# Attention by one query block of a pair of heads, with float32 value products and shortened low-part products

## Chip, cores and metric

The kernel runs on one core of a Trainium2 chip. The metric is the device time of one execution in microseconds. Five engines work side by side, each through its own queue in order: PE (matrix products; PEld is its loading of the stationary operand), DVE (elementwise and scans, also out of PSUM), ACT (activations and copies), POOL (elementwise on SBUF) and SP (here it only issues DMAs).

## What is computed

One layer of a hybrid encoder on 2048 tokens of width 1024, in float32: a norm, one input projection whose columns feed an attention group and a recurrent group, an output projection, a gated FFN with a convolution. 16 learned tokens are put before the sequence (T = 2064). The change touches the attention, for 8 heads of 64:

```python
z = einsum("bhqd,bhkd->bhqk", qb, kb) * scale
mask = s_pos < t_pos
log_keep = where(mask, log_sigmoid(-z), 0.0)
after = cumsum(log_keep, axis=3, reverse=True) - log_keep
w = where(mask, exp(log_sigmoid(z) + after), 0.0)
out = einsum("bhqk,bhkd->bhqd", w, vb)
```

## The kernel before, in words

The time axis is cut into a block of 16 tokens and 16 blocks of 128. Most products split a float32 operand into a high and a low part of the type fp32r and multiply the parts in single passes: `mm3` (L107) is high·high, high·low and low·high.

- **Projections.** For each pair of heads j, q and k go to DRAM as parts (`qd`, `kd`: the first index is high or low), v as float32 (`vd`).
- **Load of a head** (`load_head`, L115). Rows 0 to 63 of `K2` hold the high part of k, rows 64 to 127 the low part. A weight w is the difference of two neighbouring running products of keep probabilities, so the kernel multiplies the running products by differences of neighbouring v rows and adds one row of v at the end (L594). `dv` holds these differences, split by POOL into a high and a low half (L136, L137).
- **Query-key products** (`products_of`, L555). A unit is a pair of query blocks of one head. `q2` holds q twice, in both halves of the rows, so one product over 128 rows multiplies a part of q with high and low k together: L569 for the high part of q, L570 for the low part. A chunk is at most 512 keys. ACT turns it into keep probabilities (L571); DVE forms their running product backwards over one or two chunks (L578 with the mask, L580 without).
- **Value products** (`outputs_of`, `flush`, L600 to L642). PE transposes blocks of 128 x 128 (`transpose`, L97) into PSUM, two query blocks beside each other. For each group of up to 512 columns ACT copies the high part (L585) and DVE subtracts it to get the low part (L586). Each 128 keys need two products of up to 256 columns (L612), with high and low `dv` side by side in the 128 columns of the stationary operand. The two halves of the result are stored apart (`od`, L596) and are added later in `mix` (L526).
- **Order.** Units come in the order of L661, the products of one unit ahead of the outputs of the unit before. A scheduler orders each engine's queue when the program is built; the queues then run in that order. PSUM has three banks `m` for query-key products, one `v` for outputs, and two each of `t` and `u` for transposes.
- **After the attention** come the output projection with `mix` (L521, L767) and the FFN (L876 and the products L108 to L110 into `bk`).

Of the kernel before, what the change touches and what calls it, by code (L numbers as in the profile page):

```python
# [16 lines left out]
P = 128  # L17
META = 16
# [37 lines left out]
def hymba_block(  # L56
# [22 lines left out]
    od = {g: dram.tile([2, 4, P, META if g < 0 else 2 * P], F32, name=f"od{g + 1}") for g in range(-1, NT // 2)}  # L79
# [32 lines left out]
    heads = {}  # L112
    hb_stack = ExitStack()

    def load_head(hd, hb):  # L115
        j, hh = hd // 2, hd % 2
        rows = slice(hh * HD, hh * HD + HD)
        K2 = hb.tile([P, T], F32R, name="K2", tag="K2")
        dv = hb.tile([P, NT + 1, 2, HD], F32R, name="dv", tag="dv")
        nc.gpsimd.memset(f(dv[:, NT]), 0.0)  # L120
        cuts = [0, 4, 8, NT]
        for s0, s1 in zip(cuts, cuts[1:]):
            c0 = s0 * P + (META if s0 else 0)
            c1 = s1 * P + META
            for e in range(2):
                nc.sync.dma_start(f(K2[e * HD:(e + 1) * HD, c0:c1]), kd[j][e, rows, c0:c1])
            va = hb.tile([P, 9, HD], F32, name="va", tag="va")
            vb = hb.tile([P, 9, HD], F32, name="vb", tag="vb")
            m = s1 - s0
            for v, o in ((va, 1), (vb, 0)):  # L130
                nc.sync.dma_start(v[:, :m], vd[j][o + s0 * P:o + s1 * P, hh].rearrange("(s p) d -> p s d", p=P))
                if s1 == NT:
                    nc.sync.dma_start(v[:META, m], vd[j][o + NT * P:o + T, hh])
            parts = [(P, u, u + 4) for u in range(0, m, 4)] + ([(META, m, m + 1)] if s1 == NT else [])
            for n, u0, u1 in parts:
                nc.gpsimd.tensor_tensor(vb[:n, u0:u1], vb[:n, u0:u1], va[:n, u0:u1], op=ALU.subtract)  # L136
                split_pool(dv[:n, s0 + u0:s0 + u1, 0], dv[:n, s0 + u0:s0 + u1, 1], vb[:n, u0:u1])  # L137

        vl = hb.tile([NT + 1, HD], F32, name="vl", tag="vl")
        nc.sync.dma_start(vl[0:1], vd[j][META:META + 1, hh])  # L140
        nc.sync.dma_start(vl[1:], vd[j][META + P:1 + T:P, hh])
        vlT = hb.tile([P, NT + 1], F32, name="vlT", tag="vlT")
        nc.gpsimd.memset(vlT[HD:], 0.0)
        return j, rows, K2, dv, vlT, vl
# [24 lines left out]
    with ExitStack() as A:  # L169
# [332 lines left out]
        def before(j, i):  # L502
            if j == 2 and i == 0:
                heads[0] = load_head(0, hbE)
# [16 lines left out]
    def mix(mH, mL, src, t0, n):  # L521

        g, c0 = (-1, 0) if t0 < META else divmod(t0 - META, 2 * P)
        for a, d in enumerate((od[g][0, :, :, c0:c0 + n], od[g][1, :, :, c0:c0 + n], old[:, :, t0:t0 + n])):
            nc.sync.dma_start(src[a], d.rearrange("k p t -> p k t"))
        nc.vector.tensor_tensor(src[0], src[0], src[1], op=ALU.add)  # L526
        for ks, m in ((slice(0, 4), src[0]), (slice(4, 8), src[2])):
            nc.scalar.copy(mH[:, ks], m)
            nc.vector.tensor_tensor(mL[:, ks], m, f(mH[:, ks]), op=ALU.subtract)
# [4 lines left out]
    with ExitStack() as B:  # L534
# [10 lines left out]
        G = 2  # L545
        LOW = META + 8 * P

        def load_q(head, t0, n):
            j, rows = head[:2]
            q2 = hq.tile([P, 2, G * P], F32R, name="q2", tag="q2", bufs=4)  # L550
            for e in range(2):
                nc.sync.dma_start(f(q2[e * HD:(e + 1) * HD, :, :n]), qd[j][:, rows, t0:t0 + n].rearrange("s d t -> d s t"))
            return q2

        def products_of(head, i, q2, qc):  # L555

            K2 = head[2]
# [3 lines left out]
            kp = (wl if low else wk).tile([P, (LOW if low else T) + 112], F32, name="kp", tag="kp", bufs=4)  # L561
            if i >= 0:
                nc.gpsimd.memset(kp[:, n:n + 112], 0.0)  # L563
            sizes = chunks_of(n)
            hi = n
            for ci, sz in enumerate(sizes):
                c0 = hi - sz if ci == 0 else c0 - sz
                zt = acc_bank()
                nc.tensor.matmul(zt[:rn, :sz], lhsT=q2[:, 0, qc:qc + rn], rhs=K2[:, c0:c0 + sz], start=True, stop=False)  # L569
                nc.tensor.matmul(zt[:rn, :sz], lhsT=q2[:, 1, qc:qc + rn], rhs=K2[:, c0:c0 + sz], start=False, stop=True)  # L570
                nc.scalar.activation(kp[:rn, c0:c0 + sz], zt[:rn, :sz], AF.Sigmoid, scale=-0.125)  # L571
                if ci % 2 and c0:
                    continue
                rev = kp[:rn, c0:hi][:, ::-1]
                if hi == n:

                    m0 = 512 - P + rn - sz
                    nc.vector.tensor_tensor_scan(rev, rev, mask[:rn, m0:m0 + sz][:, ::-1], initial=1.0, op0=ALU.mult, op1=ALU.max)  # L578
                else:
                    nc.vector.tensor_tensor_scan(rev, rev, rev, initial=kp[:rn, hi:hi + 1], op0=ALU.mult, op1=ALU.bypass)  # L580
                hi = c0
            return kp

        def evac(h, l, src):
            nc.scalar.copy(h, src)  # L585
            nc.vector.tensor_tensor(l, src, f(h), op=ALU.subtract)  # L586

        def store_o(head, av, i0, t0, m):
            j, rows, vlT = head[0], head[1], head[4]
            ov = a1.tile([P, G * P], F32, name="qn", tag="qn", bufs=2)  # L590
            for c in range(0, m, P):
                e = min(c + P, m)
                b = i0 + 1 + c // P
                nc.scalar.activation(ov[:, c:e], av[:, c:e], AF.Identity, bias=vlT[:, b:b + 1])  # L594
            for a in range(2):
                nc.sync.dma_start(od[i0 // G][a, j, rows, :m], ov[a * HD:(a + 1) * HD, :m])  # L596
# [3 lines left out]
        def flush(head, av, pend, cols, pt, nj):  # L600
            dv = head[3]
            nflush[0] += 1
            if nflush[0] % 2:
                tH = a1.tile([P, 2, 256], F32R, name="qk", tag="qk", bufs=2).rearrange("p a t -> p (a t)")
            else:
                tH = wk.tile([P, 512], F32R, name="tH", tag="tH", bufs=2)
            tL = wk.tile([P, 512], F32R, name="tL", tag="tL", bufs=4)
            pp = pend[0][2]
# [7 lines left out]
        def outputs_of(head, g, kps):  # L616
            if g < 0:
                pt = tu_bank()
                transpose(pt[:META, :META], kps[0][:META, :META])
                av = pmv.tile([P, 2, 256], F32, name="v", tag="v")[:, 0]  # L620
                flush(head, av, [(0, 0, META, 0, META)], META, pt, 1)
                store_o(head, av, -1, 0, META)
                return
            i0 = g * G
            av = pmv.tile([P, 2, 256], F32, name="v", tag="v")[:, 0]
            nj = i0 + G + 1
            pend, cols = [], 0
            pt = tu_bank()
            for s in range(nj):
                first = max(0, s - 1 - i0)  # L630
                nn = (G - first) * P
                if cols + nn > 512:
                    flush(head, av, pend, cols, pt, nj)
                    pt = tu_bank()
                    pend, cols = [], 0
                for b in range(first, G):
                    c = cols + (b - first) * P
                    transpose(pt[:, c:c + P], kps[b][:, s * P:(s + 1) * P])
                pend.append((s, first * P, P, cols, nn))
                cols += nn  # L640
            flush(head, av, pend, cols, pt, nj)
            store_o(head, av, i0, META + i0 * P, G * P)  # L642

        def make_products(head, g):
            if g < 0:
                return [products_of(head, -1, load_q(head, 0, META), 0)]
            q2 = load_q(head, META + g * G * P, G * P)
            return [products_of(head, g * G + b, q2, b * P) for b in range(G)]
# [3 lines left out]


        def finish_head(head):

            vlT, vl = head[4:]
            pt = tu_bank()
            transpose(pt[:HD, :NT + 1], vl)
            nc.vector.tensor_copy(vlT[:HD], pt[:HD, :NT + 1])
# [354 lines left out]
```

## Time and profile before

| what | value |
|---|---|
| runs of the kernel before | 2718.18, 2722.47, 2722.88 us (median 2722.47) |
| profiled execution: its own time / its span | 2722.01 us / 2720.3 us |
| busy over the span: PE, PEld, DVE, ACT, POOL | 94%, 84%, 66%, 46%, 44% |
| mean granted clock of TensorE | 0.981 of 2.4 GHz |
| first to last scan of the attention (L578, L580) | starts from 583.3 to 1110.3 us |
| last value product (L612) starts | 1126.1 us |

The page's line of 40 slices shows which engine is full in which stage: PE in the projections and in the FFN, DVE with a 9 in every slice from the ninth to the sixteenth, which is the attention. A matmul's shown duration reaches from its start to its modelled end, and the next one starts before that; the distance between two starts is what one costs in a row.

### The profile page before, as it was taken

The page shows a single profiled execution, that of the slowest core. Times are in us where ns is not written, and L with a number is a line of the kernel's source. Part 1 is how long each engine was busy: PE and PEld are TensorE (multiplying, and loading weights), DVE is VectorE, ACT ScalarE, POOL GpSimd, SP SyncE. Part 2 cuts the span into 40 slices and gives each one's busy share as a digit, 9 for nine tenths or more (in the row PEclk, how much of TensorE's full clock was granted, in tenths as well). Part 3 has the DMA queues.
Part 4 walks back from the last instruction along what each step waited for, and adds up shares of the span by engine and source line. Part 5 has one row for each costly group of instructions (what it writes and reads, how often), then busy time and mean ns, then how long its engine had stood idle before and what let it go on. Part 6 is the DMA issues. An engine that isn't in the chain of part 4 may idle for free. (4 is left out here: it accounts for less than half of the span.)

```text
span 2720.3 us, 40399 instructions
## 1 busy us (share of the span) xinstructions
PE 2563.3 (94%) x15012; PEld 2293.5 (84%) x15012; DVE 1802.9 (66%) x2080; ACT 1241.5 (46%) x2331; POOL 1185.4 (44%) x1152
## 2 busy tenths in 40 slices
PE   7998889988888888999899999999999999999999
PEld 6998889977777778788799999988788888887887
DVE  5678853259999999655677667553745666665443
ACT  4355532246666666432355454432434545453221
POOL 4455564434522321000265555534456665653443
PEclk9999989999999999999899999999999999999999
DMA  5311143243333321577322222244653222225463
GB/s 157 111 33 33 45 113 98 76 113 96 102 81 85 83 78 50 138 222 223 108 86 71 91 74 78 86 159 146 208 169 109 79 84 79 85 79 172 141 211 109
DMA packets 316860, 296.41 MB, mean 109 GB/s; under 512 B 62182, under 2 KB 269270, under 8 KB 316662
## 3 DMA queue, kind: packets, MB, share of 16 engines
q1 hardware_dynamic: 316662, 293.82, 35.5%
q8 instruction: 118, 1.93, 0.3%
q14 instruction: 80, 0.66, 0.1%
HBM read 211.68 MB, written 82.07 MB: 108 GB/s over the span
## 5 line engine op out<-in xcount | busy, mean ns | idle before, releaser
L876 PE MATMUL bk<-mb,wt 128*128 128x258 f32 (+2 forms) x5544 | 878.8, 321 | 11.5 <-ACT u L906 2.3
L876 PEld LDWEIGHTS bk<-mb,wt 128*128 128x128 f32 x5544 | 794.9, 190 | 95.4 <-DVE c L910 3.2
L705 POOL TENSOR_TENSOR wt<-wst,wt 128x512 fp32r<-128x512 f32 (+1 forms) x264 | 485.5, 1845 | 488.8 <-ACT wt L704 263.6
L705 DVE TENSOR_TENSOR wt<-t,wt 128x512 fp32r<-128x512 f32 x88 | 173.4, 1973 | 213.0 <-ACT wt L704 213.0
L108 PE MATMUL bk<-wt 128*128 128x512 f32 x704 | 276.4, 394 | 8.0 <-ACT wt L704 8.0
L109 PE MATMUL bk<-wt 128*128 128x512 f32 x704 | 276.6, 393 | 0.0
L110 PE MATMUL bk<-wt 128*128 128x512 f32 x704 | 271.9, 391 | 4.2 <-DVE wt L705 4.2
L704 ACT CAST wt<-wst 128x512 fp32r<-128x512 f32 (+1 forms) x264 | 200.1, 762 | 121.3 <-PE bk L876 111.8
L705 POOL TENSOR_TENSOR wt<-ss,wt 128x512 fp32r<-128x512 f32 x132 | 197.0, 1495 | 121.7 <-ACT wt L704 120.4
L580 DVE TENSOR_TENSOR_SCAN kp<-kp 128x456 f32<-128x456 f32 (+6 forms) x144 | 238.2, 1655 | 0.9
L612 PE MATMUL v<-tL,dv 128*128 128x256 f32 (+1 forms) x648 | 178.7, 300 | 43.5 <-DVE tL L586 42.4
L938 DVE SCALAR_TENSOR_TENSOR t<-c,fw,t 128x1024 f32<-128x1024 f32 x88 | 135.1, 1535 | 116.0 <-ACT t L937 116.0
L571 ACT ACTIVATE kp<-m 128x388 f32<-128x388 f32 (+13 forms) x360 | 169.0, 508 | 70.7 <-PE m L570 39.7
L704 ACT CAST wt<-t 128x512 fp32r<-128x512 f32 x88 | 54.6, 621 | 281.2 <-PE bk L110 231.4
L612 PEld LDWEIGHTS v<-tL,dv 128*128 128x128 f32 x648 | 125.6, 194 | 59.1 <-DVE tL L586 57.4
L108 PEld LDWEIGHTS bk<-wt 128*128 128x128 f32 x704 | 133.9, 190 | 37.0 <-ACT wt L704 9.0
L110 PEld LDWEIGHTS bk<-wt 128*128 128x128 f32 x704 | 132.8, 189 | 33.0 <-DVE wt L705 5.5
L109 PEld LDWEIGHTS bk<-wt 128*128 128x128 f32 x704 | 133.9, 190 | 27.9
L940 DVE SCALAR_TENSOR_TENSOR c<-c,fw,t 128x1024 f32<-128x1024 f32 x88 | 154.0, 1750 | 3.0
L563 POOL MEMSET kp<- 128x112 f32 x128 | 23.7, 190 | 285.0 <-PE t L97 130.9
L569 PE MATMUL m<-K,q 128*128 128x452 f32 (+12 forms) x360 | 143.2, 399 | 2.5 <-ACT kp L571 2.2
L578 DVE TENSOR_TENSOR_SCAN kp<-kp,mask 128x388 f32<-128x388 f32 (+15 forms) x136 | 130.3, 968 | 0.1
(300 smaller groups left out, 5508.1 us busy)
## 6 DMA issues: line engine op xcount, KB each, us to landing
wst<-in_w_ffn_in_dram SPq DMA_DIRECT2D x88, 512.0 KB, 4.1
wst<-in_w_ffn_out_dram SPq DMA_DIRECT2D x88, 512.0 KB, 5.4
pd<-c SPq DMA_DIRECT2D x44, 512.0 KB, 3.3
t<-pd SPq DMA_DIRECT2D x88, 256.0 KB, 3.5
q<-qd SPq DMA_DIRECT2D x128, 128.0 KB, 2.8
wst<-in_w_in_dram SPq DMA_DIRECT2D x48, 192.0 KB, 2.8
xt<-in_x_dram SPq DMA_DIRECT2D x16, 512.0 KB
od<-qn SPq DMA_DIRECT2D x128, 64.0 KB, 2.1
```

What stands on the lines that cost most here:

```text
L108: nc.tensor.matmul(ps, lhsT=sH, rhs=mH, start=first, stop=False)
L109: nc.tensor.matmul(ps, lhsT=sH, rhs=mL, start=False, stop=False)
L110: nc.tensor.matmul(ps, lhsT=sL, rhs=mH, start=False, stop=last)
L569: nc.tensor.matmul(zt[:rn, :sz], lhsT=q2[:, 0, qc:qc + rn], rhs=K2[:, c0:c0 + sz], start=True, stop=False)
L571: nc.scalar.activation(kp[:rn, c0:c0 + sz], zt[:rn, :sz], AF.Sigmoid, scale=-0.125)
L580: nc.vector.tensor_tensor_scan(rev, rev, rev, initial=kp[:rn, hi:hi + 1], op0=ALU.mult, op1=ALU.bypass)
L612: nc.tensor.matmul(av[:, q0:q0 + nn], lhsT=dv[:pp, s].rearrange("p a d -> p (a d)"), rhs=tt[:pp, c:c + nn], start=(s == 0 and half == 0), ...
L704: nc.scalar.copy(h, src)
L705: low.tensor_tensor(l, src, f(h), op=ALU.subtract)
L876: nc.tensor.matmul(ps_, lhsT=s, rhs=m, start=first and k == 0 and n_ == 0, stop=k == 3 and n_ == 2, skip_group_check=True)
L938: nc.vector.scalar_tensor_tensor(t, c_[:, HALO - 1:HALO - 1 + PHW], pf[:, 1:2], t, op0=ALU.mult, op1=ALU.add)
L940: nc.vector.scalar_tensor_tensor(c_[:, uv], c_[:, uv], pf[:, 0:1], t, op0=ALU.mult, op1=ALU.add)
```

## The change

It has five parts.

1. A unit is one query block of a pair of heads. `load_pair` makes two tiles `K2[e]`, one per head: for head 0 the high part of k lies in rows 0 to 63, for head 1 in rows 64 to 127, the low part in the other half.
2. The high part of q still meets both parts of k over 128 rows. The low part of q meets the high part of k alone, over 64 rows: rows 0 to 63 for head 0, rows 64 to 127 for head 1 (L572). The product of the two low parts is left out.
3. The transposed products are copied as float32, by ACT or, for the second head of each fifth group, by DVE. There is no low part, and the subtract L586 is gone.
4. `dv` stays float32 and is not split. A value product has a stationary operand of 64 columns and 128 moving columns, both float32: head 0 writes partitions 0 to 63 of the bank, head 1 partitions 64 to 127 (L611).
5. The output is whole, so it is stored once per unit, and `mix` loads one table less and adds nothing.

```diff
+        K2 = [hb.tile([P, T], F32R, name=f"K2{e}", tag=f"K2{e}") for e in range(2)]
+        dv = hb.tile([P, NT + 1, 2, HD], F32, name="dv", tag="dv")
...
             for e in range(2):
-                nc.sync.dma_start(f(K2[e * HD:(e + 1) * HD, c0:c1]), kd[j][e, rows, c0:c1])
...
+                for a in range(2):
+                    nc.sync.dma_start(f(K2[e][a * HD:(a + 1) * HD, c0:c1]), kd[j][a ^ e, e * HD:(e + 1) * HD, c0:c1])
...
-                split_pool(dv[:n, s0 + u0:s0 + u1, 0], dv[:n, s0 + u0:s0 + u1, 1], vb[:n, u0:u1])
...
+                nc.gpsimd.tensor_tensor(dv[:, u:u + 4], dv[:, u:u + 4], va, op=ALU.subtract)
...
-                zt = acc_bank()
-                nc.tensor.matmul(zt[:rn, :sz], lhsT=q2[:, 0, qc:qc + rn], rhs=K2[:, c0:c0 + sz], start=True, stop=False)
-                nc.tensor.matmul(zt[:rn, :sz], lhsT=q2[:, 1, qc:qc + rn], rhs=K2[:, c0:c0 + sz], start=False, stop=True)
-                nc.scalar.activation(kp[:rn, c0:c0 + sz], zt[:rn, :sz], AF.Sigmoid, scale=-0.125)
...
+                zt = [acc_bank()[:rn, :sz] for e in range(2)]
+                for e in range(2):
+                    nc.tensor.matmul(zt[e], lhsT=q2[e][:, 0], rhs=K2[e][:, cs], start=True, stop=False)
+
+                for e in range(2):
+                    r = slice(e * HD, (e + 1) * HD)
+                    nc.tensor.matmul(zt[e], lhsT=q2[e][r, 1], rhs=K2[e][r, cs], start=False, stop=True)
+                for e in range(2):
+                    nc.scalar.activation(kps[e][:rn, cs], zt[e], AF.Sigmoid, scale=-0.125)
...
-            evac(tH[:pp, :cols], tL[:pp, :cols], pt[:pp, :cols])
-            for s, q0, pp, c, nn in pend:
-                for half, tt in enumerate((tH, tL)):
                     nc.tensor.matmul(
-                        av[:, q0:q0 + nn], lhsT=dv[:pp, s].rearrange("p a d -> p (a d)"), rhs=tt[:pp, c:c + nn],
-                        start=(s == 0 and half == 0), stop=(s == nj - 1 and half == 1))
...
+                if e and nflush[0] % 5 == 1:
+                    nc.vector.tensor_copy(tT[:pp, :cols], pts[e][:pp, :cols])
+                else:
+                    nc.scalar.copy(tT[:pp, :cols], pts[e][:pp, :cols])
+                ts.append(tT)
+            for s, nn in pend:
+                c = s % 4 * P
+                for e in range(2):
+                    nc.tensor.matmul(
+                        av[e * HD:(e + 1) * HD], lhsT=dv[:pp, s, e], rhs=ts[e][:pp, c:c + nn],
+                        start=s == 0, stop=s == nj - 1)
...
+        order = (7, 15, -1, 0, 14, 1, 13, 2, 12, 3, 11, 4, 10, 5, 9, 6, 8)
```

The scheduler builds new queues from this, and the two changes of PE's queue and the one of DVE's that matter look as follows. A row has the line, the operation, output<-inputs, and for a product stationary columns x moving columns; `v` is the output bank, `m` a bank of query-key products, `t` and `u` banks of transposes, `tH`, `tL`, `tT` and `qk` the tables copied from them.

PE in the middle of the attention before, around the last value products of a unit:

```order
L612 MATMUL v_7984<-tL_7991,dv_7557 128x256
L612 MATMUL v_7984<-qk_8000,dv_7557 128x128
L612 MATMUL v_7984<-tL_8001,dv_7557 128x128
L569 MATMUL m_8377<-K2_7556,q2_8355 128x392
L570 MATMUL m_8377<-K2_7556,q2_8355 128x392
L97 MATMUL u_8122<-ident_85,kp_8014 128x128
L97 MATMUL u_8122<-ident_85,kp_8035 128x128
```

PE in the middle of the attention of the change, value products of two groups (`tT_7678` is head 0's table, `tT_7680` and `qk_7658` are head 1's):

```order
L611 MATMUL v_7601<-qk_7658,dv_6351 64x128
L611 MATMUL v_7601<-tT_7678,dv_6351 64x128
L97 MATMUL u_7691<-ident_93,kp_7553 128x128
L611 MATMUL v_7601<-tT_7680,dv_6351 64x128
L611 MATMUL v_7601<-tT_7678,dv_6351 64x128
```

A high and a low table stood in turn, each with 128 stationary columns; now the tables of the two heads stand in turn, each with 64.

PE a little further on in the change, query-key products (`K20` is head 0's, `K21` head 1's):

```order
L572 MATMUL m_8005<-K20_6349,q2_7995 128x452
L572 MATMUL m_8006<-K21_6350,q2_7998 128x452
L611 MATMUL v_7601<-qk_7694,dv_6351 64x128
L97 MATMUL t_7822<-ident_93,kp_7779 128x128 x3
L611 MATMUL v_7601<-qk_7696,dv_6351 64x128
L97 MATMUL u_7757<-ident_93,kp_7743 128x128 x2
L97 MATMUL t_7822<-ident_93,kp_7779 128x128
L97 MATMUL u_7823<-ident_93,kp_7781 128x128 x4
L568 MATMUL m_8015<-K20_6349,q2_7995 128x452
L572 MATMUL m_8015<-K20_6349,q2_7995 128x452
L568 MATMUL m_8016<-K21_6350,q2_7998 128x452
L572 MATMUL m_8016<-K21_6350,q2_7998 128x452
```

The low-part products (L572) of the two heads stand behind one another in the first two rows and apart in the last four. Over the whole queue they stand behind one another for 56 of the 180 pairs of chunks.

DVE in the middle of the attention before (the scans L578 and L580, in the change L582 and L585, are the rows with SCALAR_TENSOR_TENSOR on `kp`):

```order
L586 TENSOR_TENSOR tL_6246<-t_6240,tH_6245 128x512
L586 TENSOR_TENSOR tL_6259<-u_6253,qk_6258 128x512
L580 SCALAR_TENSOR_TENSOR kp_6542<-kp_6542 128x392
L586 TENSOR_TENSOR tL_6272<-t_6266,tH_6271 128x512
L586 TENSOR_TENSOR tL_6285<-u_6279,qk_6284 128x512
L578 SCALAR_TENSOR_TENSOR kp_6610<-kp_6610,mask_5831 128x388
L586 TENSOR_TENSOR tL_6298<-t_6292,tH_6297 128x512
L580 SCALAR_TENSOR_TENSOR kp_6610<-kp_6610 128x780
```

DVE in the attention of the change:

```order
L585 SCALAR_TENSOR_TENSOR kp_6988<-kp_6988 128x950
L604 COPY qk_6955<-t_6944 128x512
L585 SCALAR_TENSOR_TENSOR kp_6990<-kp_6990 128x950
L582 SCALAR_TENSOR_TENSOR kp_7096<-kp_7096,mask_5836 128x392
L582 SCALAR_TENSOR_TENSOR kp_7098<-kp_7098,mask_5836 128x392
L585 SCALAR_TENSOR_TENSOR kp_7096<-kp_7096 128x392
L585 SCALAR_TENSOR_TENSOR kp_7098<-kp_7098 128x392
```

The scans are the same ones, 280 in all with the same lengths; of 360 subtracts (L586) none is left, and 36 plain copies (L604) have come.

## Rows read from the trace of the kernel before

**Rows 1.** Busy time by stage: attention, then output projection (x: instructions)
```profile
core 0: us, PE busy (x) PEld busy (x) DVE busy (x) ACT busy (x) POOL busy (x), PEclk, DMA share, GB/s
584.00:1116.00 532.00, 453.75 (x3158) 409.09 (x3157) 530.25 (x649) 351.10 (x842) 170.25 (x270) 0.96 0.33 84
...
1126.00:1294.00 168.00, 168.00 (x798) 137.38 (x797) 86.96 (x125) 48.07 (x81) 11.92 (x28) 1.00 0.76 228
```

**Rows 2.** Groups of instructions on DVE, 584 to 1126 us
```profile
L580 DVE TENSOR_TENSOR_SCAN kp<-kp 128x456 f32<-128x456 f32 (+6 forms) x144 | 238.2, 1655 | 0.9
L578 DVE TENSOR_TENSOR_SCAN kp<-kp,mask 128x388 f32<-128x388 f32 (+15 forms) x136 | 130.3, 968 | 0.1
L586 DVE TENSOR_TENSOR tL<-t,qk 128x512 fp32r<-128x512 f32 (+1 forms) x91 | 56.0, 615 | 2.4 <-ACT qk L585 1.8
```

**Rows 3.** DVE in order of time (start us, us, engine, line, operation), inside attention
```profile
906.00 0.66 DVE L586 TENSOR_TENSOR tL<-t,tH 128x512 fp32r<-128x512 f32 x1
906.59 0.68 DVE L586 TENSOR_TENSOR tL<-u,qk 128x512 fp32r<-128x512 f32 x1
```

**Rows 4.** PE in order of time, inside attention
```profile
1095.79 0.28 PE L612 MATMUL v<-qk,dv 128*128 128x256 f32 x1
1095.91 0.28 PE L612 MATMUL v<-tL,dv 128*128 128x256 f32 x1
...
1096.27 0.22 PE L612 MATMUL v<-tH,dv 128*128 128x128 f32 x1
1096.33 0.28 PE L612 MATMUL v<-tL,dv 128*128 128x128 f32 x1
...
1097.12 0.66 PE L97 MATMUL u<-ident,kp 128*128 128x128 f32 x4
1097.53 0.42 PE L569 MATMUL m<-K,q 128*128 128x388 f32 x1
1097.79 0.33 PE L570 MATMUL m<-K,q 128*128 128x388 f32 x1
1097.96 0.34 PE L569 MATMUL m<-K,q 128*128 128x390 f32 x1
```

**Rows 5.** Who waited for whom, 584 to 1126 us (total us, times, longest)
```profile
PE v L612 <- DVE tL L586: 42.4, 47, 5.0
...
PE u L97 <- DVE tL L586: 23.6, 23, 2.4
```

**Rows 6.** Page, costliest groups: value products, query-key products, sigmoids
```profile
L612 PE MATMUL v<-tL,dv 128*128 128x256 f32 (+1 forms) x648 | 178.7, 300 | 43.5 <-DVE tL L586 42.4
...
L571 ACT ACTIVATE kp<-m 128x388 f32<-128x388 f32 (+13 forms) x360 | 169.0, 508 | 70.7 <-PE m L570 39.7
...
L569 PE MATMUL m<-K,q 128*128 128x452 f32 (+12 forms) x360 | 143.2, 399 | 2.5 <-ACT kp L571 2.2
```

**Rows 7.** Groups of instructions on ACT, 584 to 1126 us
```profile
L585 ACT CAST qk<-t 128x512 fp32r<-128x512 f32 (+1 forms) x91 | 49.8, 550 | 34.7 <-PE t L97 23.5 <-PE v L612 10.3 <-DVE tL L586 0.5
...
L594 ACT ACTIVATE qn<-v,vlT 128x128 f32<-128x128 f32 (+1 forms) x134 | 42.1, 368 | 5.7 <-DMA q<-qd 3.2 <-PE v L612 2.3
```

**Rows 8.** Groups on DVE in the output projection, a plain copy and the sum
```profile
L526 DVE TENSOR_TENSOR m<-m,m 128x512 f32<-128x512 f32 x15 | 10.4, 690 | 15.2 <-DMA m<-od 10.4 <-issue 4.4
...
L812 DVE COPY sT<-u 128x512 f32<-128x512 f32 (+1 forms) x13 | 8.4, 647 | 0.0
```

**Rows 9.** PE in order of time, start of the output projection
```profile
1132.69 0.40 PE L103 MATMUL pu<-woH,mM 128*48 128x512 f32 x1
1132.93 0.39 PE L105 MATMUL pu<-woL,mM 128*16 128x512 f32 x1
...
1133.38 0.39 PE L103 MATMUL pu<-woH,mM 128*48 128x512 f32 x1
1133.61 0.39 PE L108 MATMUL pu<-woH,mB 128*128 128x512 f32 x1
```

More of the change, by code (lines that the diff above doesn't have):

```diff
@@ L78, in hymba_block @@
     vd = [dram.tile([1 + T, 2, HD], F32, name=f"vd{j}") for j in range(4)]
-    od = {g: dram.tile([2, 4, P, META if g < 0 else 2 * P], F32, name=f"od{g + 1}") for g in range(-1, NT // 2)}
+    od = [dram.tile([4, P, META if i < 0 else P], F32, name=f"od{i + 1}") for i in range(-1, NT)]
     old = dram.tile([4, P, T], F32, name="old")
@@ L110, in mm3, with load_pair @@
         nc.tensor.matmul(ps, lhsT=sL, rhs=mH, start=False, stop=last)
-    heads = {}
+    pairs = {}
     hb_stack = ExitStack()
[L115 to L120, printed above, removed]
+    def load_pair(j, hb):
+        K2 = [hb.tile([P, T], F32R, name=f"K2{e}", tag=f"K2{e}") for e in range(2)]
+        dv = hb.tile([P, NT + 1, 2, HD], F32, name="dv", tag="dv")
+        nc.gpsimd.memset(dv[:, NT], 0.0)
         cuts = [0, 4, 8, NT]
@@ L125, in load_head @@
             for e in range(2):
[L126 to L128 removed]
+                for a in range(2):
+                    nc.sync.dma_start(f(K2[e][a * HD:(a + 1) * HD, c0:c1]), kd[j][a ^ e, e * HD:(e + 1) * HD, c0:c1])
             m = s1 - s0
[L130 to L136, printed above, removed]
[L137 to L141 removed]
+            for u in range(s0, s1, 4):
+                va = a1.tile([P, 4, 2, HD], F32, name="vt", tag="vt", bufs=2)
+                for v, o in ((va, 1), (dv[:, u:u + 4], 0)):
+                    nc.sync.dma_start(v, vd[j][o + u * P:o + (u + 4) * P].rearrange("(s p) h d -> p s h d", p=P))
+                nc.gpsimd.tensor_tensor(dv[:, u:u + 4], dv[:, u:u + 4], va, op=ALU.subtract)
+        va = a1.tile([P, 4, 2, HD], F32, name="vt", tag="vt", bufs=2)
+        for v, o in ((va[:META, 0], 1), (dv[:META, NT], 0)):
+            nc.sync.dma_start(v, vd[j][o + NT * P:o + T])
+        nc.gpsimd.tensor_tensor(dv[:META, NT], dv[:META, NT], va[:META, 0], op=ALU.subtract)
+        vl = hb.tile([NT + 1, P], F32, name="vl", tag="vl")
+        nc.sync.dma_start(vl[0:1], vd[j][META:META + 1].rearrange("o h d -> o (h d)"))
+        nc.sync.dma_start(vl[1:], vd[j][META + P:1 + T:P].rearrange("o h d -> o (h d)"))
         vlT = hb.tile([P, NT + 1], F32, name="vlT", tag="vlT")
[L143 to L144 removed]
+        return j, K2, dv, vlT, vl
     ps_mv = ExitStack()
@@ L503, in before @@
             if j == 2 and i == 0:
-                heads[0] = load_head(0, hbE)
+                pairs[0] = load_pair(0, hbE)
         qkv_run([1, 2, 3], w, before, None, A.close)
@@ L544, in hymba_block, with load_q, products_of @@
         )
-        G = 2
         LOW = META + 8 * P
[L548 to L552, printed above, removed]
-            return q2
-        def products_of(head, i, q2, qc):
-            K2 = head[2]
+        def load_q(pair, e, t0, n):
+            j = pair[0]
+            q2 = (hq, wk)[e].tile([P, 2, P], F32R, name="q2", tag="q2", bufs=4)[:, :, :n]
+            for a in range(2):
+                nc.sync.dma_start(
+                    f(q2[a * HD:(a + 1) * HD]), qd[j][:, e * HD:(e + 1) * HD, t0:t0 + n].rearrange("s d t -> d s t"))
+            return q2
+        def products_of(K2, i, q2):
             rn, t0 = (META, 0) if i < 0 else (P, META + i * P)
@@ L575, in products_of @@
-                if hi == n:
-                    m0 = 512 - P + rn - sz
-                    nc.vector.tensor_tensor_scan(rev, rev, mask[:rn, m0:m0 + sz][:, ::-1], initial=1.0, op0=ALU.mult, op1=ALU.max)
-                else:
[L580 to L596, printed above, removed]
@@ L616, in outputs_of @@
[L616 to L648, printed above, removed]
+                for kp in kps:
+                    rev = kp[:rn, c0:hi][:, ::-1]
+                    if hi == n:
+                        m0 = 512 - P + rn - sz
+                        nc.vector.tensor_tensor_scan(
+                            rev, rev, mask[:rn, m0:m0 + sz][:, ::-1], initial=1.0, op0=ALU.mult, op1=ALU.max)
+                    else:
+                        nc.vector.tensor_tensor_scan(
+                            rev, rev, rev, initial=kp[:rn, hi:hi + 1], op0=ALU.mult, op1=ALU.bypass)
@@ new lines, in products_of, with flush @@
+                hi = c0
+            return kps
+        nflush = [0]
+        def flush(pair, av, pend, pp, pts, nj):
+            dv = pair[2]
+            nflush[0] += 1
+            cols = sum(nn for s, nn in pend)
+            ts = []
+            for e in range(2):
+                if nflush[0] % 2:
+                    tT = f(a1.tile([P, 2, 256], F32R, name="qk", tag="qk", bufs=2).rearrange("p a t -> p (a t)"))
+                else:
+                    tT = wk.tile([P, 512], F32, name="tT", tag="tT", bufs=4)
+                if e and nflush[0] % 5 == 1:
+                    nc.vector.tensor_copy(tT[:pp, :cols], pts[e][:pp, :cols])
+                else:
+                    nc.scalar.copy(tT[:pp, :cols], pts[e][:pp, :cols])
+                ts.append(tT)
+            for s, nn in pend:
+                c = s % 4 * P
+                for e in range(2):
+                    nc.tensor.matmul(
+                        av[e * HD:(e + 1) * HD], lhsT=dv[:pp, s, e], rhs=ts[e][:pp, c:c + nn],
+                        start=s == 0, stop=s == nj - 1)
@@ new lines, in outputs_of @@
+        def outputs_of(pair, i, kps):
+            j, vlT = pair[0], pair[3]
+            n, nj = (META, 1) if i < 0 else (P, i + 2)
+            av = pmv.tile([P, 512], F32, name="v", tag="v")[:, :n]
+            for s0 in range(0, nj, 4):
+                blocks = range(s0, min(s0 + 4, nj))
+                pts = [tu_bank() for e in range(2)]
+                for e in range(2):
+                    for s in blocks:
+                        transpose(pts[e][:n, (s - s0) * P:(s - s0) * P + n], kps[e][:n, s * P:s * P + n])
+                flush(pair, av, [(s, n) for s in blocks], n, pts, nj)
+            ov = a1.tile([P, 256], F32, name="qn", tag="qn", bufs=2)
+            nc.scalar.activation(ov[:, :n], av, AF.Identity, bias=vlT[:, i + 1:i + 2])
+            nc.sync.dma_start(od[i + 1][j], ov[:, :n])
@@ L650, in staging, with make_products, finish_pair @@
+        def make_products(pair, i):
+            t0, n = (0, META) if i < 0 else (META + i * P, P)
+            return products_of(pair[1], i, [load_q(pair, e, t0, n) for e in range(2)])
         def staging():
             return a1.tile([P, 4, 2, HD], F32, name="vt", tag="vt", bufs=2).rearrange("p a b d -> p (a b d)")
-        def finish_head(head):
-            vlT, vl = head[4:]
+        def finish_pair(pair):
+            vlT, vl = pair[3:]
             pt = tu_bank()
-            transpose(pt[:HD, :NT + 1], vl)
-            nc.vector.tensor_copy(vlT[:HD], pt[:HD, :NT + 1])
@@ L661, in hymba_block @@
-        units = [(hd, g) for hd in range(HEADS) for g in (3, 7, -1, 0, 6, 1, 5, 2, 4)]
+            transpose(pt[:, :NT + 1], vl)
+            nc.vector.tensor_copy(vlT, pt[:, :NT + 1])
+        order = (7, 15, -1, 0, 14, 1, 13, 2, 12, 3, 11, 4, 10, 5, 9, 6, 8)
+        units = [(j, g) for j in range(4) for g in order]
         late = []
-        seen = set()
-        for n, (hd, g) in enumerate(units):
-            if hd not in heads:
-                heads[hd] = load_head(hd, (hbE, hbO)[hd % 2])
-            if hd not in seen:
-                seen.add(hd)
-                finish_head(heads[hd])
+        for n, (j, g) in enumerate(units):
+            if g == order[0]:
+                finish_pair(pairs[j])
@@ L670, in hymba_block @@
             if late:
                 outputs_of(*late.pop(0))
-            kps = make_products(heads[hd], g)
-            late.append((heads[hd], g, kps))
+            if g == 13 and j < 3:
+                pairs[j + 1] = load_pair(j + 1, (hbO, hbE)[j % 2])
+            kps = make_products(pairs[j], g)
+            late.append((pairs[j], g, kps))
             k = n - (len(units) - 2 * KD)
@@ L767, in mixed @@
             def mixed(i):
-                src = [cp.tile([P, 4, P], F32, name=f"m{a}", tag=f"m{a}", bufs=1) for a in range(3)]
+                src = [cp.tile([P, 4, P], F32, name=f"m{a}", tag=f"m{a}", bufs=1) for a in range(2)]
                 mix(*(mA, mB)[i % 2], src, META + (i - 1) * P, P)
```

28 lines of the change are left out of this document (9 added, 19 removed).

## Prediction

> **What bounds the kernel now.** I read the page's 40 slices first, then busy time by stage, then DVE's groups, then who waits for whom, and last PE's rows one by one for the distance between starts.
>
> The stage that the change touches runs from 584 to 1126 us. In its first 532 us DVE is busy for 530.25 us, PE for 453.75 and ACT for 351.10 [rows 1]. So DVE sets the pace, with no idle time worth naming before its scans [rows 2]. PE waits for DVE: 42.4 us before value products and 23.6 us before transposes, both for the low part that L586 writes [rows 5]. In the output projection that follows, PE is busy for all of its 168 us [rows 1]. A microsecond saved in the attention therefore reaches the end as it is, and one saved on another engine behind it is worth nothing.
>
> **DVE.** The four groups of L586 like the one shown [rows 2] hold 360 subtracts: 288 of 512 columns, 64 of 128 and 8 of 16. Shown durations overlap, so I price by starts: the next instruction begins 0.59 us after a subtract of 512 columns [rows 3]. For the small ones I take the columns in proportion, 0.15 and 0.02. That is 288 x 0.59 + 64 x 0.15 + 8 x 0.02 = 180 us. It all goes. What is left of 530 is 350 us, nearly all scans, which stay as they are. 36 copies come, 32 of them of 512 columns; a plain copy out of PSUM of that size shows 647 ns [rows 8] against 615 mean of the subtracts [rows 2], so 0.59 each, 20 us. DVE then needs **370 us**.
>
> **ACT.** 36 of 360 copies move to DVE (550 ns each [rows 7], -20 us). The biased output copy L594 is issued once per unit instead of twice, 68 for 136 (368 ns [rows 7], -25 us). ACT needs about **306 us** of today's 351.
>
> **PE.** Transposes stay: about 1220 blocks of 128 x 128. Four of them are followed by the next product after 0.41 us, and that one takes 0.26 instead of 0.17 [rows 4], so 0.10 to 0.125 each; at 0.11 it is **135 us**. Query-key products cost 0.17 to 0.18 at 390 columns [rows 4]. 360 of them for the high part of q [rows 6] stay, 63 us. The 360 for the low part keep their columns and lose half their rows; rows do not enter the price if they run alone, so they cost 63 us again, unless the two heads' halves run at the same time. The queue puts them next to each other for 56 of 180 pairs only, so the saving is between 0 and 56 x 0.175 = 10 us. I take 10: **116 us** in all.
>
> The value products are the term that decides, and no row shows one like them. Before, 1296 products: 0.12 at 256 columns and from 0.06 at 128 [rows 4], 147 us in all. Now there are 1224, of 128 columns, float32 on both sides. From below, one costs 0.06, as a 128-column product of parts does [rows 4]. From above, a product exact in both operands is what four products of parts give (the three of `mm3` and low by low), so 4 x 128 = 512 columns, and a 512-column product takes 0.23 [rows 9]. I take 0.23, since float32 without splitting is the reason why four terms are needed. The second unknown is whether the two heads, which use different halves of the columns and of the bank, run at once. If so, 612 pairs x 0.23 = **141 us**; if not, 282. I take 141: the queue has the heads in turn nearly everywhere, nothing they read or write is shared, and the pairs are what this order makes possible. From below, 1224 x 0.06 = 73 us.
>
> A price that only a page states: the Trainium skill, "FP8 and Floating Point Precision" (TensorE Precision Notes), counts four passes for true FP32. By it the term would be the upper price, 0.23.
>
> PE's sum is 135 + 116 + 141 = **392 us**, against 408 on the same prices before.
>
> **What is hidden.** POOL loses the splits of `dv` (L92, L93); it is busy for 170 of 532 us [rows 1], so nothing. SP issues 272 loads of q for 144 and 68 stores for 144, loads of k 48 for 48, of v 48 for 80; with `mix` 470 in all against 467, so its queue is as long as before and no load is moved behind more than it had. The 17 adds of L526 (690 ns [rows 8]) and a third of `mix`'s loads lie beside a PE that is full [rows 1]: nothing. If that cover went, it would be at most 17 x 0.69 = 12 us.
>
> **The sum.** After the change PE needs 392, DVE 370 and ACT 306 us. Three queues in order that feed each other in a ring, this close together, do not run without gaps. PE idles for 532 - 454 = 78 us now, 66 of it for L586 [rows 1, 5]. I give it half of 78, so the stage lasts 431 us instead of 532: 101 us less. The tail to 1126 stays. Against the profiled execution's own 2722.01 us this is **2621 us**; the median of the runs is 2722.47, half a microsecond away. With no gaps it is 2582, with 85 us of gaps 2667: the forecast's own range.
>
> **Rivals.**
>
> 1. *The halves do not run at once.* Every value product then stands alone: 282 us, and the low parts cost 126 with the high ones. PE needs 135 + 126 + 282 = 543 us, more than the whole stage now. With the 12 us of PE idle time that L586 does not explain, the stage is 555 and the time **2745 us**: slower. It decides from a pair price of (520 - 251) / 612 = 0.44 us upwards. For it: no row of this kernel shows two products at once. Against it: disjoint columns.
> 2. *The array has to empty when the shape changes.* The new queue changes 883 times between full products, those over 64 rows and those with 64 columns. A product of 128 columns shows 0.22 to 0.28 us from start to end while the next can start after 0.06 [rows 4], so emptying could cost 0.16 each time, 141 us: PE 533, with the same 12 us a stage of 545, **2735 us**: slower. Against it stand the products with 48 and 16 columns, which alternate with each other and with 128 at 0.23 to 0.24 us each, without a visible pause [rows 9]; but these all start at column 0. The Trainium skill, "TensorEngine Tiling (Array Packing)" (Key Properties), says that a change of tiling mode drains the engine, while tiles of one mode work in parallel; by that rule the heads would run at once and the drain would be paid, 2735, where the rows without a pause give 2621. The trace shows no drain so far as rows 9 reach.
> 3. *A new wait for banks.* A pair of chunks takes two of three `m` banks, and a sigmoid costs 508 ns [rows 6]. Where nothing stands between, two sigmoids take about 0.96 us and four products 0.70, so up to 0.26 x 180 = 47 us more: stage 478, **2668 us**. For it: ACT already idles 70.7 us before sigmoids, 39.7 of it for products [rows 6]. Against it: transposes and value products stand in most of these places.
> 4. *Float32 is cheap.* At 0.06 PE needs 324 us, DVE's 370 bound, with 10 us of gaps the stage is 380 and the time **2570 us**.
>
> That the subtracts do not go is excluded: the new queue has none.
>
> **Chances.** Forecast 0.57, rival 1 0.17, rival 2 0.09, rival 3 0.12, rival 4 0.05. A measurement of this kernel tells 0.2% (5.4 us) from no change. The forecast, 3 and 4 are faster, 0.74, and parts of a drain or of an overlap still leave something: 0.04 more, so 0.78. Same 0.04. Slower 0.18. The range runs from rival 4, 2570, to rival 2, 2735, and leaves out most of rival 1.
>
> **What would show it.** Right: L611 pairs 0.23 us apart, their two starts a few hundredths apart; DVE below full in the attention, with PE the fullest; the output projection starting near 1025 us. DVE's L604 at 20 us and no L586 tests the first term. Wrong: each L611 0.2 us or more after the one before (rival 1); gaps of 0.16 before and after each run of L572 or L611 (rival 2); PE idle for L574's sigmoid before L568 (rival 3); DVE still at its full share (rival 4).

## The result, and the profile after

The change is slower: 2742.51 us (median of 4 runs, 2739.34 to 2746.04) against 2721.44 us for the kernel before (4 runs beside them), ratio 1.008 [1.0067, 1.0092]. The prediction was 2621 us. The profiled execution took 2746.04 us (before: 2722.01 us).

Busy time by stage of the change, the attention and then the output projection, with the columns of [rows 1]:

```profile
core 0: us, PE busy (x) PEld busy (x) DVE busy (x) ACT busy (x) POOL busy (x), PEclk, DMA share, GB/s
584.00:1116.00 532.00, 531.55 (x4085) 371.88 (x4085) 354.43 (x314) 320.94 (x712) 97.95 (x169) 0.96 0.28 73
1152.00:1320.00 168.00, 168.00 (x795) 138.03 (x794) 78.56 (x111) 47.78 (x80) 11.27 (x28) 1.00 0.67 201
```

DVE fell from 530.25 to 354.43 us in a stretch of the same length. PE rose from 453.75 to 531.55, which is all of the stretch. PE took DVE's place as the bound and needs longer than DVE did: from the first query-key product to the last value product the stage lasts 571 us (578.7 to 1149.8), before 546 (579.8 to 1126.1). The 25 us more are the whole difference of the two profiled executions (24 us); the output projection behind them is full on PE as before.

Groups of DVE in the change, 580 to 1160 us, beside [rows 2], then who waited for whom, beside [rows 5] (total us, times, longest):

```profile
L585 DVE TENSOR_TENSOR_SCAN kp<-kp 128x694 f32<-128x694 f32 (+11 forms) x144 | 230.5, 1639 | 114.9 <-ACT kp L574 114.7
L582 DVE TENSOR_TENSOR_SCAN kp<-kp,mask 128x388 f32<-128x388 f32 (+15 forms) x136 | 123.6, 945 | 28.3 <-ACT kp L574 28.3
L604 DVE COPY tT<-u 128x512 f32<-128x512 f32 x10 | 6.9, 686 | 14.0 <-PE u L97 14.0
```

```profile
DVE kp L585 <- ACT kp L574: 114.7, 58, 7.0
ACT kp L574 <- PE m L572: 91.9, 191, 1.7
PEld m L572 <- issue: 59.9, 267, 0.4
```

The scans cost what they did, but stand idle for 143 us where they had 1 us. DVE waits for sigmoids, the sigmoids for the low-part product L572, and L572's load of its stationary operand stands for 0.2 us on average (59.9 / 267) with nothing to wait for.

PE row by row in the change (start us, us, engine, line), where [rows 4] had starts 0.17 us apart at 390 columns:

```profile
636.86 0.55 PE L97 MATMUL t<-ident,kp 128*128 128x128 f32 x3
637.16 0.45 PE L568 MATMUL m<-K,q 128*128 128x452 f32 x1
637.55 0.47 PE L572 MATMUL m<-K,q 64*128 64x452 f32 x1
637.94 0.63 PE L568 MATMUL m<-K,q 128*128 128x400 f32 x2
638.50 0.45 PE L572 MATMUL m<-K,q 64*128 64x400 f32 x2
638.88 0.43 PE L611 MATMUL v<-qk,dv 128*64 128x128 f32 x2
639.25 0.26 PE L97 MATMUL u<-ident,vt 44*128 44x44 f32 x1
639.43 0.98 PE L611 MATMUL v<-qk,dv 128*64 128x128 f32 x13
```

Three things stand here. From L568 to L572 and from L572 to the next it takes 0.39 us each, where 452 columns at 2.4 GHz take 0.19: 0.2 us is lost both times. The two L572 of 638.50 together take 0.38 us until the next product, no more than one alone: the halves of the rows do run at once, but pay the pause too. And L611 x2, one float32 product, takes 0.37 us until the small transpose, where it needs 0.22 inside a run.

I counted the distance from start to start beyond the columns at 2.4 GHz for every two neighbours on PE between 584 and 1152 us of the change:

```
from -> to                                    count   median us beyond the columns
128 rows, 128 columns -> 64 rows               287     0.204
64 rows -> 128 rows, 128 columns               222     0.208
64 rows -> 64 columns                           66     0.208
64 columns -> 128 columns                      159     0.150
128 columns -> 64 columns                      102     0.150
same shape, head 0 and 1 low part in turn       56     second starts 3 ns after the first
```

With a few small shapes that is 598 changes of rows at 0.206, 123 us, and 272 changes of columns at 0.15, 41 us: **164 us** that PE spends on changing its shape. This is an estimate and not a net price. Where the same neighbours have one shape, a step also takes 0.018 us (query-key products in e1) or 0.056 to 0.059 us (transposes and value products in e5) beyond its columns, which makes 26 us for so many. Against that, the first transpose behind a change takes 0.112 us instead of 0.056, which the count leaves out.

The groups that answer to [rows 6] and [rows 7], 580 to 1160 us:

```profile
L568 PE MATMUL m<-K,q 128*128 128x452 f32 (+12 forms) x359 | 146.0, 433 | 2.3 <-DMA q<-qd 1.8 <-ACT kp L574 0.3
L572 PE MATMUL m<-K,q 64*128 64x452 f32 (+12 forms) x359 | 137.1, 453 | 0.0
L611 PE MATMUL v<-qk,dv 128*64 128x128 f32 x1224 | 105.3, 281 | 0.0
```

The mean of L568 has grown from the 399 ns of L569 [rows 6] with the same columns, and L572, with half the rows, shows more still. L611 has 2448 records in two groups for 1224 products: a float32 product shows as two, each 0.109 us.

### The profile page after: what moved, and what is told of

It is laid out like the page before. It is cut to its first block, busy times and chain, and to the rows that moved or that the text cites. A ratio compares the mean times of both kernels' runs of the same rounds, so it can differ in the third digit from the quotient of the medians.

```text
span 2744.3 us, 41954 instructions
## 1 busy us (share of the span) xinstructions
PE 2663.4 (97%) x16160; PEld 2270.3 (83%) x16160; DVE 1628.5 (59%) x1735; ACT 1224.8 (45%) x2227; POOL 1108.9 (40%) x1040
## 5 line engine op out<-in xcount | busy, mean ns | idle before, releaser
L585 DVE TENSOR_TENSOR_SCAN kp<-kp 128x694 f32<-128x694 f32 (+11 forms) x144 | 230.5, 1639 | 114.9 <-ACT kp L574 114.7
L574 ACT ACTIVATE kp<-m 128x452 f32<-128x452 f32 (+12 forms) x360 | 170.3, 501 | 94.8 <-PE m L572 91.9
L568 PE MATMUL m<-K,q 128*128 128x452 f32 (+12 forms) x360 | 146.4, 433 | 2.3 <-DMA q<-qd 1.8
L582 DVE TENSOR_TENSOR_SCAN kp<-kp,mask 128x388 f32<-128x388 f32 (+15 forms) x136 | 123.6, 945 | 28.3 <-ACT kp L574 28.3
L572 PE MATMUL m<-K,q 64*128 64x452 f32 (+12 forms) x360 | 137.5, 452 | 0.0
L687 ACT CAST wt<-ss 128x512 fp32r<-128x512 f32 x132 | 81.9, 622 | 82.7 <-PE bk L859 73.2
```

Source lines behind the costliest of these rows:

```text
L568: nc.tensor.matmul(zt[e], lhsT=q2[e][:, 0], rhs=K2[e][:, cs], start=True, stop=False)
L572: nc.tensor.matmul(zt[e], lhsT=q2[e][r, 1], rhs=K2[e][r, cs], start=False, stop=True)
L574: nc.scalar.activation(kps[e][:rn, cs], zt[e], AF.Sigmoid, scale=-0.125)
```

## The experiments

**Theory A**: a change of shape on PE costs 0.15 us (columns) or 0.2 us (rows) each time, and the halves of the columns run at once. **Theory B**: the halves do not run at once, and the value products themselves are dear (rival 1). Lines shift by one where an experiment takes one out.

**e1: low products over all rows.** No change of rows is left; the product of the low parts comes back.

```diff
-                    r = slice(e * HD, (e + 1) * HD)
-                    nc.tensor.matmul(zt[e], lhsT=q2[e][r, 1], rhs=K2[e][r, cs], start=False, stop=True)
+                    nc.tensor.matmul(zt[e], lhsT=q2[e][:, 1], rhs=K2[e][:, cs], start=False, stop=True)
```

> The changed kernel with one edit: the low part of q is multiplied with both parts of k over all 128 rows, as before the change. Theory A (a change of the array's shape empties PE): the trace of the change shows 0.21 us extra at each of some 598 changes into and out of products over 64 rows, 123 us; the 56 pairs that ran at once cost 10 us more when they stand alone, so 113 us go and the time is about 2630 us. Rival B (the float32 value products and their copies set the stage, whatever the rows): within 10 us of the change's 2742.

Measured: 2668.09 us, ratio 0.9803 [0.9788, 0.9818]; 74 us less than the change by an edit that gives PE more to multiply. PE in e1, and then busy time by stage:

```profile
700.27 0.66 PE L97 MATMUL t<-ident,kp 128*128 128x128 f32 x4
700.69 0.41 PE L568 MATMUL m<-K,q 128*128 128x346 f32 x1
700.93 0.33 PE L571 MATMUL m<-K,q 128*128 128x346 f32 x1
701.09 0.32 PE L568 MATMUL m<-K,q 128*128 128x346 f32 x1
701.25 0.32 PE L571 MATMUL m<-K,q 128*128 128x346 f32 x1
```

```profile
584.00:1040.00 456.00, 436.21 (x4081) 364.49 (x4081) 355.78 (x311) 303.73 (x711) 101.12 (x169) 1.00 0.34 85
```

Products of 346 columns now start 0.16 us apart, high and low alike, without a pause. I added up the distances from each start on PE to the next (PE's distances, below), from the first query-key product to the last value product. Query-key products take 241 us of the change's stage and 163 of e1's, value products 173 and 171, transposes 157 and 158. So the whole saving lies with the products whose rows were edited, 78 us in the two profiled executions.

That is less than the 113 us that A expected. The trace shows what comes back: PE is no longer full, it idles for 22 us of the stage instead of 2; where a value product followed a 64-row one, a change of columns stays (64 times 0.108, 7 us); and like neighbours take 0.018 us each beyond their columns (some 530 more of them, 10 us). The ring of waits takes its share again: DVE still waits for sigmoids, 53.6 us before L584, and ACT for value products, 40.7. The granted clock was at its lower level, half of full speed, for 41 us of the change's stage and for 7 us of e1's, which can be worth 17 of the 78 us at most.

**e2: the kernel before with half-height low products.** One line; the product of the low parts is left out.

```diff
-                nc.tensor.matmul(zt[:rn, :sz], lhsT=q2[:, 1, qc:qc + rn], rhs=K2[:, c0:c0 + sz], start=False, stop=True)
+                nc.tensor.matmul(zt[:rn, :sz], lhsT=q2[:HD, 1, qc:qc + rn], rhs=K2[:HD, c0:c0 + sz], start=False, stop=True)
```

> The kernel before with one edit: the low part of q meets the high part of k alone, over rows 0 to 63 (the product of the two low parts is left out). Theory A: up to 360 low-part products stand alone, 720 changes of shape at 0.21 us, 148 us on PE, which needs 408 + 148 = 556 us against DVE's 530: slower, 2750 to 2780 us. Rival B (rows cost nothing by themselves): the time of before, 2721, within 6 us.

Measured: 2762.85 us, ratio 1.0142 [1.0115, 1.0168], inside the expectation. PE in e2:

```profile
709.80 0.44 PE L569 MATMUL m<-K,q 128*128 128x388 f32 x1
710.17 0.44 PE L570 MATMUL m<-K,q 64*128 64x388 f32 x1
710.53 0.66 PE L97 MATMUL t<-ident,kp 128*128 128x128 f32 x4
```

In [rows 4] the step from one such product to the next is 0.17 us, or 0.26 right behind transposes; here both steps take 0.37 and 0.36. The float32 value products and the pairing of heads are not in this kernel, so the pause belongs to the half height alone: 346 changes into it at 0.194 us and 336 out at 0.208, some 137 us in all. Only 41 reach the end, since the kernel before had DVE as its bound and PE waiting beside it: PE idles for 79 us of the stage before and for 7 in e2. The granted clock fell in most runs of e2 as well (0.975 in the profiled one, 0.981 before); the one run of e2 at 0.984 took 2751.46 us, which is still 30 us over the median before.

**e3: head 1's value product first.** e1 with the two heads' value products in the other order within each pair; by the queue this makes longer runs of one shape.

```diff
-                for e in range(2):
+                for e in (1, 0):
```

> The first experiment with one more edit: of each block's two value products the second head's is issued first. Its table is copied last, so the queue no longer starts a group with a single product and breaks off: 125 runs of value products in the queue instead of 170. Theory A: 90 changes between 64 and 128 columns fewer at 0.15 us, 13 us less than the first experiment, about 2617 us. Rival B: no change from the first experiment.

Measured: 2661.55 us (2654.81 to 2662.15), ratio 0.9769 [0.9748, 0.979]: 6.5 us less than e1, half of what was expected. 89 changes of columns are gone from the trace, 13 us at 0.15, and PE idles some 9 us more instead. It is the fastest of all versions here, 60 us under the kernel before.

**e4: value products of the heads apart.** e1 with all value products of head 0 in a group before those of head 1.

```diff
-            for s, nn in pend:
-                c = s % 4 * P
-                for e in range(2):
+            for e in range(2):
+                for s, nn in pend:
+                    c = s % 4 * P
```

> The first experiment with one more edit: the value products of a group go first for head 0, then for head 1, not in turn. If the two heads run at once only because they stand in turn (theory A's other half), a pair costs 0.44 us instead of 0.22, 612 pairs cost 133 us more, and the time is about 2760 us. If the halves of the columns never ran at once, or run at once in any order, the time is that of the first experiment.

Measured: 2708.14 us, ratio 0.9948 [0.9931, 0.9964]: 40 us more than e1, not 133. PE in e4, where the queue has eight records (four products) of head 1 from the table `tT`, then eight of head 0 from the next group's table `qk`:

```profile
704.21 0.76 PE L610 MATMUL v<-tT,dv 128*64 128x128 f32 x5
704.70 0.32 PE L610 MATMUL v<-qk,dv 128*64 128x128 f32 x1
704.80 0.27 PE L610 MATMUL v<-tT,dv 128*64 128x128 f32 x1
704.86 0.27 PE L610 MATMUL v<-qk,dv 128*64 128x128 f32 x1
704.91 0.27 PE L610 MATMUL v<-tT,dv 128*64 128x128 f32 x1
```

Five records of head 1 start about 0.1 us apart (0.109 behind the first), so alone a product of two records takes 0.218 us, what a pair takes in e1; then head 0's first one starts while three of head 1, ahead of it in the queue, are still to come, and the two go on beside each other. So the first few run alone and the rest at once, and the overlap does not need the heads to be strictly in turn. Theory A survives; my reading that PE starts its products strictly by the queue does not.

**e5: value products with 128 stationary columns.** e1 with the differences of both heads side by side in the stationary operand; each head keeps its own half of the result. No product has another shape.

```diff
-                        av[e * HD:(e + 1) * HD], lhsT=dv[:pp, s, e], rhs=ts[e][:pp, c:c + nn],
-                        start=s == 0, stop=s == nj - 1)
+                        av[:, e * P:e * P + nn], lhsT=dv[:pp, s].rearrange("p a d -> p (a d)"), rhs=ts[e][:pp, c:c + nn],
+                        start=s == 0 and e == 0, stop=s == nj - 1 and e == 1)
...
-            nc.scalar.activation(ov[:, :n], av, AF.Identity, bias=vlT[:, i + 1:i + 2])
+            for e in range(2):
+                r = slice(e * HD, (e + 1) * HD)
+                nc.scalar.activation(ov[r, :n], av[r, e * P:e * P + n], AF.Identity, bias=vlT[r, i + 1:i + 2])
```

> As e1 (low products over 128 rows, 2668 us), and every value product has 128 stationary columns: the differences of v of both heads side by side. Head 0's product is kept from columns 0 to 127 of the bank, head 1's from columns 128 to 255, in the half of the partitions that belongs to each head, and the output is taken off by two activations of 64 partitions. No product of the attention has another shape than 128 x 128 now. Theory A (the halves run at once; a change between 128 and 64 stationary columns costs about 0.15 us): the 340 changes go, 51 us less, but a pair of float32 products takes 2 x 0.218 instead of 0.218 us, 612 x 0.218 = 133 us more: about 2750 us. Rival B (that a pair takes 0.218 us has nothing to do with the halves; a float32 product takes 0.109): only the changes go, about 2617 us. Trace by A: value products 0.218 us apart start to start, none beside another, and no pause before or after a run of them; by B: 0.109 apart.

Measured: 2752.63 us, ratio 1.0111 [1.0091, 1.0131], as theory A has it. Sixteen records of L610 on PE, first with 64 columns (e3), then with 128 (e5):

```profile
701.93 1.09 PE L610 MATMUL v<-qk,dv 128*64 128x128 f32 x16
702.96 0.66 PE L97 MATMUL t<-ident,kp 128*128 128x128 f32 x4
```

```profile
702.95 1.95 PE L610 MATMUL v<-tT,dv 128*128 128x128 f32 x16
704.74 1.50 PE L610 MATMUL v<-qk,dv 128*128 128x128 f32 x12
```

Both are eight products, four per head: 1.03 us against 1.79 until the next group begins. Without the change of shape of 0.15 us the first is 0.88, eight steps of 0.11 for sixteen records; the second is sixteen steps. The halves of the columns do run at once, and here that is worth more than the changes of shape it costs.

**e7 and e8: all low products in pairs.** In e7 the two query-key banks of a pair of heads are one tile, so the scheduler gets both at the same time and all 180 pairs of half-height products stand together. The banks differ from the change (the tile of `m` twice, one bank `u` instead of two); e8 has the same banks and full-height low products.

```diff
-                zt = [acc_bank()[:rn, :sz] for e in range(2)]
+                zz = pmv.tile([P, 2, 512], F32, name="m", tag="m", bufs=2)
+                zt = [zz[:rn, e, :sz] for e in range(2)]
```

> The change itself, with the two query-key banks of a pair of heads taken together as one tile (two pairs of banks instead of three single banks; the output bank moves to the transposes' pool, which gives one up). By that all 180 pairs of 64-row products stand behind one another in PE's queue (56 before); the queue has 360 changes to or from 64 rows (608 before) and 538 between 128 and 64 columns (276 before). Theory A (0.206 us for a change of rows, 0.15 of columns, 64-row pairs at once): 248 x 0.206 = 51 us less, 262 x 0.15 = 39 more, 124 more pairs at once x 0.175 = 22 less: 34 us less than the change, about 2708, and up to 30 more if single banks make new waits. Against its control e8 (below): 360 x 0.206 = 74 us more, 56 fewer column changes x 0.15 = 8 less, 180 x 0.175 = 31 less: 35 us slower than e8. Rival B (a pair pays once its two products stand together): 31 us faster than e8.

> Control of e7: the same banks, but the low-part products over all 128 rows as in e1. No change of rows in the queue, 594 changes between 128 and 64 columns (340 in e1). Theory A: e1's 2668 us + 254 x 0.15 = 38 us, about 2706, and 35 us faster than e7. Rival B (column changes cost nothing, only row changes do): 2668 us as e1, but for waits on the banks. Rival C (a 64-row pair pays when it stands together): 31 us slower than e7.

Measured: e7 2742.48 us, ratio 1.0078 [1.0061, 1.0095]; e8 2730.14 us, ratio 1.0031 [1.0021, 1.0041]. Pairs that always stand together are still 12 us slower than full-height products; A said 35 slower, rivals B and C 31 faster. PE in e7, then in e8, at the same chunks:

```profile
703.96 0.63 PE L569 MATMUL m<-K,q 128*128 128x412 f32 x2
704.52 0.46 PE L573 MATMUL m<-K,q 64*128 64x412 f32 x2
704.91 0.66 PE L97 MATMUL u<-ident,kp 128*128 128x128 f32 x4
```

```profile
704.00 0.54 PE L569 MATMUL m<-K,q 128*128 128x412 f32 x2
704.37 0.54 PE L572 MATMUL m<-K,q 128*128 128x412 f32 x2
704.75 0.60 PE L97 MATMUL u<-ident,kp 128*128 128x128 f32 x4
```

Four products take 0.95 us with halves at once and 0.75 without. A's price was too high on one side: in e7 the change into half height shows 0.105 us in the median, not 0.204; out of it 0.21 as ever. The change itself shows both: 0.209 (225 times) when the product just before is the high one for the same bank, 0.108 (50 times) when it is the other head's.

The bank differs between these, but the rows point elsewhere: the first full-height product behind other work is dear by itself. Behind transposes its distance to the second is 0.10 us beyond its columns even in e8, where no row changes (0.015 for those after it), and behind a half-height pair it is 0.12 in e7. The two L569 above take 0.56 us in e7 and 0.37 in e8. Where only one full-height product stands between, as mostly in the change, this and the change into half height fall on one step: 0.19 us behind transposes, 0.21 behind half height. The change into half height itself then adds 0.09 us in both kernels. Why the first product is dear is not shown.

With 0.105 + 0.21 - 0.175 = 0.14 a pair, 180 x 0.14 = 25 us, and 8 less for columns, e7 should be 17 us behind e8; measured 12. The query-key products alone take 173 us of PE's distances in e7 and 160 in e8, and PE idles for 14 us of the stage in e7 and for 25 in e8.

e8 stands 62 us behind e1 instead of 38. The column changes are there (566 between 64 and 128 columns, at 0.15). The rest came with the banks too, the only edit between the two, and hardly as idle time (25 us against 22): value products take 215 us of PE's distances where e1 has 171, transposes 177 where it has 158. In e7 the query-key products save 68 us against the change (241 to 173), near the 73 that A expected, and value products and transposes lose 37 and 20 us where A had 39 for both. So e7 comes out equal to the change, which A had 34 us above it before waits on the banks.

## Why the prediction was wrong, step by step

- **DVE** was right: subtracts gone, scans unchanged, 373 us busy from 584 to 1150 us for 370 forecast. **ACT** was 35 us too low, 341 for 306, and it does not matter while PE is full.
- **Value products** were right in size and in kind: 0.23 us forecast for a pair of float32 products at once, 0.218 measured (133 us instead of 141). Rival 1, the one I held likeliest after the forecast, is refuted by e5: without overlap the kernel takes 84.5 us more than e1.
- **The step that failed is the price of nothing for a change of shape on PE.** In the sum, query-key products "keep their columns and lose half their rows", and value products cost 141 us, with no term for going from one shape to another. I let [rows 9] decide: products with 48 and 16 stationary columns alternate with 128 without a pause. They do so in the change as well, but what they show does not carry over to halves of 64 rows, or of 64 columns in two places. The changes cost 164 us. Rival 2, with 0.16 each time and 2735 us, was the right mechanism with nearly the right price; I gave it 0.09. The rule of the Trainium skill that I cited there, "TensorEngine Tiling (Array Packing)" (Key Properties), says that a change of tiling mode drains the engine and that tiles of one mode work in parallel. The trace agrees with it here: a pause of 0.1 to 0.21 us at a change, and a second half that starts 3 to 7 ns after the first.
- **Saving 10 us by 56 adjacent low products**: the overlap is real (3 ns apart), but each pair pays up to 0.41 us for two changes to save 0.175.
- **39 us of gaps**: there are none. PE is busy for 531.55 of 532 us; a bound this clear waited for nobody. Where PE is less full, gaps come back, 22 us in e1. Rival 3, waits for banks, is hardly seen: L568 was held up by L574 for 0.3 us in all, its loads for 7.6.

Together: 2621 + 164 (shape) - 8 (value products) - 39 (gaps) = 2738 us, against 2742.51 measured. That it comes so near is in part luck, since the prices were not complete: they gave the kernel before 408 us of PE, whose busy time was already 453.75 [rows 1]. Told without prices, by PE's distances over the stage, query-key products took 241 us for 116 forecast, value products 173 for 141 and transposes 157 for 135. The largest of the three misses is the one that e1 takes down to 163 us by removing the changes of rows.

## What to carry to other kernels

Count the changes of shape in PE's queue before using half-height or half-width products: here each cost 0.15 us between 128 and 64 columns and 0.1 to 0.21 us between 128 and 64 rows, as much as 240 to 500 moving columns. Two halves at once pay only in runs: a run of value products saved 0.218 us a pair against up to 0.3 us for going in and out, and in none of these runs did a single pair of 400-column half-height products earn its changes. Better let the other half of the rows do needless work than reshape the array for one product.

## What the runs showed that I had not expected

- The load of the next stationary operand pauses at a change of shape as well: it stands idle for 0.2 us before L572, 267 times, with nothing to wait for; before its full-height counterpart in e1, L571, it does so once.
- 48 and 16 stationary columns cost no change, 64 columns do. The first hold parts and all start at column 0; the second are float32 and half of them start at column 64. Which of these differences decides was not tried.
- A float32 product of 128 columns shows as two records of 0.109 us, so 0.218 us, near the 0.23 of a 512-column product of parts.
- PE does not start products of different halves strictly by its queue: in e4 those of one half of the columns began while three of the other, ahead of them in the queue, were still to start.
- The first full-height query-key product behind transposes takes 0.10 us beyond its columns without any change of shape, those after it 0.015. A change into half height adds 0.09 us, a change out of it 0.19.
